# Most of the latent projection as seven half-block products, between those of the gate group, and the sums of w_out run on into the latent heads

## The chip, the core and the metric

The kernel runs on one core of a Trainium2 chip, in one launch. The metric is the device time of the whole kernel in microseconds; runs of one kernel agree within about 0.1 us here. The core has TensorE (matmuls into PSUM banks of 128 x 512 float32), VectorE, ScalarE, GpSimd (POOL in the profile) and SyncE (SP), which issues most transfers. All transfers run on the core's 16 DMA engines.

## The reference

One decoder layer on 512 tokens of width 2048: a combined input projection of the normalized x, eight latent-attention heads and eight forgetting-attention heads, gated with SiLU, an output projection and a normalized residual.

```
h = _rms_norm(x, g_pre)
proj = h @ w_in
(q_lat, kv_lat, k_rope_raw, gate_mla,
 fq, fk, fv, f_logit, gate_fox) = jnp.split(proj, split_points, axis=-1)
o_mla = _mla_branch(q_lat, kv_lat, k_rope_raw, g_q, w_uq, g_kv, w_ukv, cos, sin) * jax.nn.silu(gate_mla)
o_fox = _fox_branch(fq, fk, fv, f_logit, b_forget) * jax.nn.silu(gate_fox)
o = jnp.concatenate([o_mla, o_fox], axis=-1) @ w_out
return x + _rms_norm(o, g_post)
```

The first 768 columns of w_in give q_lat, the next 512 kv_lat. Both are RMS-normalized over their columns and go through w_uq and w_ukv to the queries, keys and values of the latent heads. Everything is float32.

## The kernel before

**Arithmetic.** Each float32 operand is split into a rounded high part (ScalarE) and the low remainder (VectorE), and a product is three matmuls: high x high, high x low, low x high (`mm3`, lines 128 to 131).

**Weights.** All weights pass through one list of chunks of 128 x 1024 values. `chunk(i)` issues the load of chunk i + 4 on SP's queue and queues the split of chunk i + 2 (`divide`, lines 227 to 235: `whi` on ScalarE, `wlo` on VectorE). There are three buffers each for the raw chunk (loads from line 221, or from line 212 for prepared sums), `whi` and `wlo`. So two chunks can stand ready ahead of TensorE and three more be loaded.

**Side work.** `todo` is a list of closures that `pump` takes from while a projection runs: `rate` closures after each block of 128 rows. `wait(n)` puts n empty ones in, `drain` empties the list. `later` is a second list, taken from at every third call of `behind`. Each engine runs its instructions in one order, which the framework's scheduler sets when the program is built, by and large that of the program.

**Seven products.** The latent heads' gate group (1024 columns, tag "m") and the output projection (two groups of 1024 columns, 0 and 1) are each computed as a 2 x 2 block product with seven half-size products, p1, p2, p4, q6, g5, g7 and g3, in the manner of Strassen and Winograd. That needs sums of weight blocks (t4 to t7) and of blocks of x (or of the heads' outputs).
- The weight sums are made by DMA alone, from DRAM to DRAM: `sum_blocks` lists them in `bg` (16 for each group), and `add_step` (lines 273 to 283) issues one step: an accumulating transfer on POOL's queue (line 278), a copy on SP's queue (line 281), and a mark of 64 bytes that ties the next step to TensorE's progress (line 283). `behind` takes a step after every `pace` row blocks of the projections that call it; 7 for the forgetting heads, 6 for the latents, 7 in the latent heads.
- The sums of x are made in `x_steps` while the forgetting heads are projected, split, and put away to DRAM on POOL's queue (`put_away`, line 841). They are fetched back on SP's queue (`fetch`, line 847) beside the product before the one that uses them (`side`).
- `product` (lines 859 to 890) runs one of the seven. The left operand (x or its sums) is the stationary side, a weight half block of 512 columns the moving one; two PSUM banks hold the 256 tokens of a half.

**Order.** (1) x is transposed and split, the forgetting heads are projected in four pairs, their attention pumped beside (up to 407 us). (2) The latents: five groups of 256 columns, plain products over 16 row blocks (`proj_T`, tile `l`, 407 to 523 us): a block of weights of 128 columns against all 512 tokens, so the result stands with columns on partitions. After each group `latent` squares and scales its two parts; after the third and the fifth `latent_scale` turns the summed squares into a row of factors, by eight small matmuls (line 1073), a square root, diagonals (lines 422 and 423), and a matmul that spreads them (lines 431 and 432); then each part is scaled (line 1087). (3) The gate group's seven products (tiles `ga` to `gd`, 523.6 to 603.7 us), the splits of the ten normalized latents pumped beside (`part_latents`, lines 1110 to 1114), then transposes of the gates (line 1147). (4) The latent heads in four pairs (from 603.7 us). (5) The output projection's fourteen products.

All these tiles of 128 x 2 x 512 live in one pool of 28 slots.

## Time and profile before

| | us |
|---|---|
| median of 3 runs | 913.7 (913.68 to 913.78) |
| profiled execution, span from first to last instruction | 912.0 |
| TensorE busy | 903.8 |
| VectorE busy | 601.1 |
| ScalarE busy | 409.3 |
| latent groups, first to last matmul | 407.2 to 523.4 |
| gate group's products, first to last matmul | 523.6 to 603.4 |

Groups of instructions stand as line, engine, operation, tiles, shapes and count, then busy us and mean ns of one, then the engine's idle time before them and what ended it. A row of the order of time is start, length, engine, line. A row of stretches has the stretch, its length, then busy us (and instructions) of TensorE, of its weight loads, VectorE, ScalarE and POOL, then the granted clock, the busy share of the DMA engines and GB/s. A row of waits is who waited for whom: total, times, longest. A row of transfers ends in KB each and the median us to landing; a row of one tile has min/median/max ns and the first and last start. Matmuls are pipelined: a row's length covers part of the next one's, so their price is the distance between starts.

### The profile page before, as it was taken

How to read it: one execution, taken by the hardware profiler on the slowest of the kernel's cores; microseconds unless marked ns; L12 is line 12 of the kernel's file. 1: busy time of each engine (PE TensorE's matmuls, PEld its weight loads, DVE VectorE, ACT ScalarE, POOL GpSimd, SP SyncE). 2: the span in 40 equal slices, each digit the busy share in tenths (PEclk: the TensorE clock that was granted, in tenths of full speed). 3: DMA queues.
4: the chain of work that ended last, by engine and by line, in shares of the span. 5: the costliest groups of instructions: out<-in, count | busy, mean ns of one | idle time of the engine just before them, and what ended most of it. 6: DMA issues, size and time to landing. Idle time of an engine off the chain costs nothing.

```text
span 912.0 us, 12253 instructions
## 1 busy us (share of the span) xinstructions
PE 903.8 (99%) x4460; PEld 767.2 (84%) x4460; DVE 601.1 (66%) x1042; ACT 409.3 (45%) x731; POOL 77.3 (8%) x101
## 2 busy tenths in 40 slices
PE   9999999999999999999999999999999999999997
PEld 8988888898889888888888888888888888888885
DVE  4477779447366674673644556778978895876686
ACT  6772434243223442342533354644454465644474
POOL 1001101011112010111220100000000000000021
PEclk9999999999999999999999999999999999999998
DMA  9368876877788878987999998877422146787868
GB/s 304 92 186 205 210 193 183 213 185 185 202 228 251 231 171 251 248 240 174 293 320 285 269 318 307 296 223 175 102 77 71 47 149 215 238 323 225 275 192 253
DMA packets 119808, 196.20 MB, mean 215 GB/s; under 512 B 15650, under 2 KB 67388, under 8 KB 119748
## 3 DMA queue, kind: packets, MB, share of 16 engines
q1 hardware_dynamic: 103556, 152.03, 50.7%
q0 software_dynamic: 15456, 43.00, 22.8%
q8 instruction: 35, 0.57, 0.2%
q10 hardware_dynamic: 736, 0.40, 0.2%
q14 instruction: 25, 0.20, 0.1%
HBM read 175.45 MB, written 70.27 MB: 269 GB/s over the span
## 4 chain that ended last, share of the span: by engine, by line
PE 94%; DMA 2%; DVE 1%; ACT 1%; issue 0%; SPq 0%; ACTq 0%
PE fv L526 4%; PE l L129 4%; PE l L131 4%; PE l L130 4%; PE fg L129 3%; PE fq L131 3%; PE fq L129 3%; PE fq L130 3%; PE fg L130 3%; PE fg L131 3%; PE fk L130 3%; PE fk L129 3%; PE fk L131 3%; PE sm L565 3%; PE fv L130 2%; PE fv L131 2%
## 5 line engine op out<-in xcount | busy, mean ns | idle before, releaser
L234 DVE TENSOR_TENSOR wlo<-raw,whi 128x1024 fp32r<-128x1024 f32 (+3 forms) x193 | 228.3, 1185 | 182.0 <-ACT whi L233 173.8
L233 ACT CAST whi<-raw 128x1024 fp32r<-128x1024 f32 (+3 forms) x193 | 197.2, 1023 | 277.2 <-PE fk L130 45.6
L129 PE MATMUL l<-h,whi 128*128 128x512 f32 x160 | 63.3, 396 | 0.0
L131 PE MATMUL l<-h,wlo 128*128 128x512 f32 x160 | 62.4, 390 | 0.0
L130 PE MATMUL l<-h,whi 128*128 128x512 f32 x160 | 62.4, 390 | 0.0
L129 PE MATMUL fq<-h,whi 128*128 128x512 f32 x128 | 52.6, 411 | 0.0
L129 PE MATMUL fg<-h,whi 128*128 128x512 f32 x128 | 50.4, 394 | 0.0
L131 PE MATMUL fq<-h,wlo 128*128 128x512 f32 x128 | 50.3, 393 | 0.0
L130 PE MATMUL fq<-h,whi 128*128 128x512 f32 x128 | 50.1, 391 | 0.0
L129 PE MATMUL fk<-h,whi 128*128 128x512 f32 x128 | 50.0, 391 | 0.0
L130 PE MATMUL fg<-h,whi 128*128 128x512 f32 x128 | 50.0, 391 | 0.0
L131 PE MATMUL fg<-h,wlo 128*128 128x512 f32 x128 | 49.9, 390 | 0.0
L130 PE MATMUL fk<-h,whi 128*128 128x512 f32 x128 | 49.8, 389 | 0.0
L131 PE MATMUL fk<-h,wlo 128*128 128x512 f32 x128 | 49.8, 389 | 0.0
L131 PE MATMUL fv<-whi,h 128*128 128x256 f32 (+1 forms) x128 | 39.5, 309 | 0.0
L130 PE MATMUL fv<-wlo,h 128*128 128x256 f32 (+1 forms) x128 | 39.5, 309 | 0.0
L129 PE MATMUL fv<-whi,h 128*128 128x256 f32 (+1 forms) x128 | 39.5, 309 | 0.0
L526 PE MATMUL fv<-whi,h 128*128 128x456 f32 x128 | 37.7, 378 | 0.0
L278 POOL DMA_DIRECT2D t<-in_w_out_dram x16 | 18.7, 1167 | 207.4 <-DMA t<-in_w_out_dram 207.1
L131 PEld LDWEIGHTS l<-h,wlo 128*128 128x128 f32 x160 | 30.0, 188 | 6.4
L129 PEld LDWEIGHTS l<-h,whi 128*128 128x128 f32 x160 | 30.0, 188 | 5.9
L130 PEld LDWEIGHTS l<-h,whi 128*128 128x128 f32 x160 | 30.1, 188 | 5.8
(473 smaller groups left out, 2208.0 us busy)
## 6 DMA issues: line engine op xcount, KB each, us to landing
raw<-in_w_in_dram SPq DMA_DIRECT2D x84, 512.0 KB
t<-in_w_out_dram SPq DMA_DIRECT2D x32, 512.0 KB
raw<-t SPq DMA_DIRECT2D x32, 512.0 KB
raw<-in_w_out_dram SPq DMA_DIRECT2D x24, 512.0 KB
t<-in_w_out_dram POOLq DMA_DIRECT2D x16, 512.0 KB, 8.0
t<-t POOLq DMA_DIRECT2D x16, 512.0 KB, 8.0
awaymg<-smg POOLq DMA_DIRECT2D x12, 512.0 KB, 7.4
bmg<-awaymg SPq DMA_DIRECT2D x12, 512.0 KB
```

Source lines behind the costliest of these rows:

```text
L129: pe.matmul(o, ah, bh, start=first, stop=False, **kw)
L130: pe.matmul(o, ah, bl, start=False, stop=False, **kw)
L131: pe.matmul(o, al, bh, start=False, stop=last, **kw)
L233: act.copy(hi[:, :m], raw[:, :m])
L234: dve.tensor_tensor(out=lo[:, :m], in0=raw[:, :m], in1=hi[:, :m].bitcast(F32), op=ALU.subtract)
L278: pool.dma_start(to.rearrange("p (k c) -> p k c", k=2), second, accum_op=ALU.add)
L526: pe.matmul(banks[t][:, :n], a[k][:, tss[t]], b[:, j, :], start=k == 0 and m == 0, stop=k == NK - 1 and m == 2,)
L565: pe.matmul(s[:, :nn], a[:, qs], c[:, :nn], start=(i == 0), stop=(i == len(pairs) - 1))
```

## The change

The first 1024 of the 1280 latent columns become a group "l" of seven products like the gate's. Its left operands are the same blocks and sums of x as the gate's, held until both groups have used them. `turned` makes the weight block of 128 columns the stationary side and 256 tokens the moving one, so that the result has columns on partitions as before. The last 256 latent columns stay a plain group and come first. p1, p2 and p4 of the two groups alternate; then q6, g5, g7, g3 of the latents run, then those of the gate. The latents' squares, statistics, rows, scalings and splits are pumped beside the latents' g3 and the gate's q6 and g5 (two closures after each block), with shorter waits between them. The list of weight sums grows by 16 steps, which come first; the pace is 6 row blocks for a step up to the plain latent group, 16 in the products (which now take steps too, through `paced`), and 2 in the latent heads. The fetches of x sums run beside p2 and q6 to g5 of the latents and p4 of the gate.

```diff
-    state = {"loaded": 0, "divided": 0, "tiles": 0, "turn": 0, "step": -1, "pace": 7}
+    state = {"loaded": 0, "divided": 0, "tiles": 0, "turn": 0, "step": -1, "pace": 6}
...
-    lat = [add_chunks(w_in, [(0, 256 * p, 256)], NK, 4, 256) for p in range(5)]
+    lat = add_chunks(w_in, [(0, 1024, 256)], NK, 4, 256)
...
+    AT = {"l": 0, "m": O_GM}
+
+    def in_block(g, j, h, c):
         k = 2 * j + 8 * h
-        return w_in[0, k * P : (k + 2) * P, O_GM + 512 * c : O_GM + 512 * (c + 1)].rearrange("(k p) c -> p k c", p=P)
-
-    sum_blocks("m", gate_block)
+        off = AT[g] + 512 * c
+        return w_in[0, k * P : (k + 2) * P, off : off + 512].rearrange("(k p) c -> p k c", p=P)
+
+    for g in "lm":
+        sum_blocks(g, lambda j, h, c, g=g: in_block(g, j, h, c))
     add_products(
-        [(n, "m") for n in ("p1", "p4", "p2", "q6", "g5", "g7", "g3")],
-        lambda g, h, c: add_chunks(w_in, [(0, O_GM + 512 * c, 512)], 8, 2, 512, 8 * h),
+        [
+            *((n, g) for n in ("p1", "p2", "p4") for g in "lm"),
+            *((n, g) for g in "lm" for n in ("q6", "g5", "g7", "g3")),
+        ],
+        lambda g, h, c: add_chunks(w_in, [(0, AT[g] + 512 * c, 512)], 8, 2, 512, 8 * h),
     )
...
+            for f in range(2):
+                c = slice((2 * t + f) * P, (2 * t + f + 1) * P)
+                mm3(
+                    o[t][:, f * HALF : (f + 1) * HALF], hi[:, j, c], lo[:, j, c], *parts(kk),
+                    first and kk == 0 and f == 0, last and kk == 7, skip_group_check=True,
+                )
...
                 pump(rate)
+                paced(hi)
...
+    def latent_row(j):
+        make_row(accs[:, j, :], f"lr{LAT[j][0]}", *lat_diag[j])
...
+    def latent_part(i):
+        j = int(i >= 6)
+        dve.tensor_tensor(out=raw(i), in0=raw(i), in1=accs[:, j, :], op=ALU.mult)
+        latents[i] = split(raw(i), f"ln{i}")
...
+    def lat_sum(to, o, add, op=ALU.add):
+        for t in range(2):
+            dve.tensor_tensor(out=to[t], in0=fold(o[t]), in1=add[t], op=op)
...
+    state["pace"] = 16
+    A, A2 = ([proj_bank(f"g{n}{t}") for t in range(2)] for n in "lm")
+    product("p1", "l", x_wide(0, 0), A, True, True, 2, turned=True)
...
+    product("p1", "m", x_block(0, 0), A2, True, True, 2)
...
+    product("p2", "l", x_wide(1, 0), A, False, True, 2, side=fetches("q6", "m"), turned=True)
...
+    product("p2", "m", x_block(1, 0), A2, False, True)
...
+    product("p4", "l", x_wide(1, 2), B, True, True, turned=True)
+    lat_sum(lat_block(0, 1), B, pl)
+    product("p4", "m", x_block(1, 2), B2, True, True, side=fetches("g5", "m"))
...
+    drain()
...
+    product("q6", "l", sums_wide("q6"), C, True, True, side=fetches("g7", "m"), turned=True)
...
+    product("g5", "l", sums_wide("g5"), G, True, True, side=fetches("g3", "m"), turned=True)
+    lat_sum(lat_block(1, 1), G, pl, ALU.subtract)
+    product("g7", "l", sums_wide("g7"), C, False, True, turned=True)
+    lat_sum(lat_block(1, 1), C, lat_block(1, 1))
+    lat_less(lat_block(0, 1), C)
+    for i in range(4):
+        todo.append(lambda i=i: latent(i, raw(i)))
+    product("g3", "l", sums_wide("g3"), G, False, True, turned=True)
+    lat_sum(lat_block(1, 0), G, lat_block(1, 0))
+    for i in range(4, 8):
+        todo.append(lambda i=i: latent(i, raw(i)))
+    wait(2)
+    todo.append(lambda: latent_stats(0))
+    todo.append(lambda: latent_stats(1))
+    wait(6)
+    todo.append(lambda: latent_row(0))
+    todo.append(lambda: latent_row(1))
+    wait(3)
+    for i in range(10):
+        todo.append(lambda i=i: latent_part(i))
+    C, G = ([proj_bank(f"g{n}m{t}") for t in range(2)] for n in "cd")
+    product("q6", "m", operand("q6", "m"), C, True, True, 2)
...
+    product("g5", "m", operand("g5", "m"), G, True, True, 2)
...
-    part_latents()
-    product("g7", "m", operand("g7", "m"), C, False, True)
+    product("g7", "m", operand("g7", "m"), C, False, True, 2)
...
-    state["pace"] = 7
+    state["pace"] = 2
```

More of the change, by code (lines that the diff above doesn't have):

```diff
@@ L857, in operand, with product @@
         return parts
-    def product(name, g, parts, o, first, last, rate=1, at=None, held=0, side=()):
+    def product(name, g, parts, o, first, last, rate=1, at=None, held=0, side=(), turned=False):
         side = deque(side)
@@ L1163, in tile_hybrid_layer @@
-    c11 = slot("gc11")
-    scaled_copy(c11, A, 0)
-    C = [proj_bank(f"gc{t}") for t in range(2)]
-    product("q6", "m", operand("q6", "m"), C, True, True, side=fetches("g7", "m"))
+    state["pace"] = 16
+    A, A2 = ([proj_bank(f"g{n}{t}") for t in range(2)] for n in "lm")
+    product("p1", "l", x_wide(0, 0), A, True, True, 2, turned=True)
+    pl = slot("lp")
+    for t in range(2):
+        act.copy(pl[:, t, :], A[t])
+    pl = [fold(pl[:, t, :]) for t in range(2)]
+    product("p1", "m", x_block(0, 0), A2, True, True, 2)
@@ L1187, in tile_hybrid_layer @@
             f()
-    qnh, qnl = zip(*qn)
-    knh, knl = zip(*kn)
+    qnh, qnl = zip(*(latents[i] for i in range(6)))
+    knh, knl = zip(*(latents[i] for i in range(6, 10)))
     for p in range(4):
```

104 lines of the change are left out of this document (54 added, 50 removed).

## The prediction

> **What bounds the kernel now.** I read the page first, then who TensorE waited for, then its order of time and the stretches around the change.
>
> ```profile
> span 912.0 us, 12253 instructions
> ...
> PE 903.8 (99%) x4460; PEld 767.2 (84%) x4460; DVE 601.1 (66%) x1042; ACT 409.3 (45%) x731; POOL 77.3 (8%) x101
> ...
> PEclk9999999999999999999999999999999999999998
> DMA  9368876877788878987999998877422146787868
> ...
> PE 94%; DMA 2%; DVE 1%; ACT 1%; issue 0%; SPq 0%; ACTq 0%
> ```
>
> TensorE is busy for 903.8 of 912.0 us at full clock, and the chain that ended last is TensorE for 94%. So the time is the sum of matmul spacings, and an edit counts by what it does to that sum or by a hole it makes in it. The list of TensorE's own waits shows how few holes there are:
>
> ```profile
> PE mix L1306 <- ACT scaler L1305: 1.9, 1, 1.9
> PE warm L148 <- DVE warm L143: 1.1, 1, 1.1
> PE xt L394 <- DMA xa<-in_x_dram: 0.6, 1, 0.6
> PE gmt L1147 <- DVE gc L1131: 0.4, 1, 0.4
> ```
>
> Between the first and the last few microseconds there is one hole, of 0.4 us, at the gate transposes. The digits of DMA say that around the latent and gate stages (slices 18 to 24, 410 to 570 us) its engines are nearly full: that is where to look for a new bound.
>
> **The matmuls removed and added.** Four of the five latent groups go: 4 groups x 16 row blocks x 2 outputs x 3 terms = 384 matmuls that stream 512 columns. Seven products come: 7 x 8 x 2 x 2 x 3 = 672 matmuls that stream 256, since turned, each weight block of 128 columns is the stationary side and half the tokens (256) the moving one. A matmul's shown length overlaps its neighbours, so the price is the distance of starts:
>
> ```profile
> 448.06 0.39 PE L129 MATMUL l<-h,whi 128*128 128x512 f32 x1
> ...
> 453.50 0.39 PE L129 MATMUL l<-h,whi 128*128 128x512 f32 x1
> ...
> 173.55 0.28 PE L129 MATMUL fv<-whi,h 128*128 128x256 f32 x1
> ...
> 196.58 0.40 PE L129 MATMUL fg<-h,whi 128*128 128x512 f32 x1
> ...
> L131 PE MATMUL fv<-whi,h 128*128 128x256 f32 x64 | 18.1, 283 | 0.0
> ...
> 419.17 0.28 PE L129 MATMUL pvf<-phf,fv0h 128*128 128x256 f32 x1
> ...
> 419.51 0.40 PE L129 MATMUL l<-h,whi 128*128 128x512 f32 x1
> ```
>
> The latent matmuls: 24 starts in 453.50 - 448.06 = 5.44 us, 0.2267 us each. The value projection of the second head pair has the very form that comes, 128 x 128 stationary and 256 moving, back to back: 3 x 64 = 192 starts in 196.58 - 173.55 = 23.03 us, 0.120 us each. That is not half of 0.2267: if 256 more columns cost 0.1067 us, each matmul pays 0.0133 us besides. So removed 384 x 0.2267 = 87.0 us, added 672 x 0.120 = 80.6 us, **gain 6.4 us**. In other words, an eighth of the streaming saved (384 x 0.2133 / 8 = 10.2 us) and 288 more fixed costs (3.8 us) paid. The bounds: three lone matmuls of 256 (419.17 to 419.51) stand 0.113 apart, which would give 672 x 0.113 = 75.9 and a gain of 11.1; no row of this form is slower than 0.120. I take 0.120, the row with 192 of them in a run.
>
> The Trainium skill, "TensorE: Matmul & The Clock Gate", section Back-to-back issue gap, has N/2.4 ns + 2.5 ns per matmul, which would price the pair at 215.8 and 109.2 ns and the gain at an estimated 9.5 us. The Trainium skill's "Perfetto Trace Analysis", section Matmuls, speaks against the edit: larger matmuls are more efficient than smaller ones. This trace agrees with that direction and has the larger price, 13.3 ns for each matmul instead of 2.5; the row decides.
>
> **Weights, splits, evacuation.** The seven products read 28 chunks of 1024 columns where 16 were read: 12 more loads of 512 KB, 12 more roundings on ScalarE and 12 more subtractions on VectorE (some 1.0 and 1.2 us each by the rows of L233 and L234 below). TensorE takes a chunk in 24 x 0.120 = 2.88 us instead of 24 x 0.2267 = 5.44. A chunk is prepared two ahead, so the two engines' 2.2 us fit into 5.8 us of lead: cost nothing, covered by TensorE's own work, and up to 12 x 2.2 = 26 us if there were no lead. The evacuations (4 copies, 12 additions of 128x512) run while the next product uses other banks: p1, p2 and p4 alternate with the gate group's, and q6, g5, g7, g3 alternate two bank pairs as the gate products do now. Nothing, but they load VectorE.
>
> **Statistics and splits of the latents, moved behind g3 into the gate group's last four products.** Here VectorE must do in 4 x 48 x 0.2267 = 43.5 us what it did over a longer stretch:
>
> ```profile
> 562.00:594.00 32.00, 32.00 (x143) 26.48 (x142) 22.45 (x26) 17.59 (x23) 0.00 (x0) 1.00 0.86 307
> 594.00:606.00 12.00, 11.64 (x61) 9.48 (x60) 10.93 (x15) 6.54 (x9) 0.00 (x0) 1.00 0.59 154
> 606.00:640.00 34.00, 34.00 (x188) 29.33 (x187) 24.64 (x45) 14.95 (x28) 1.99 (x2) 1.00 0.78 215
> ...
> L234 DVE TENSOR_TENSOR wlo<-raw,whi 128x1024 fp32r<-128x1024 f32 (+1 forms) x16 | 18.7, 1173 | 11.0 <-ACT whi L233 10.8
> L233 ACT CAST whi<-raw 128x1024 fp32r<-128x1024 f32 (+3 forms) x193 | 197.2, 1023 | 277.2 <-PE fk L130 45.6
> L1087 DVE TENSOR_TENSOR lat<-lat,ls 128x512 f32<-128x512 f32 x10 | 6.4, 688 | 0.0
> L1064 DVE TENSOR_TENSOR ls<-ls,lq 128x512 f32<-128x512 f32 x4 | 2.8, 692 | 4.0 <-ACT lq L1061 4.0
> ...
> 535.87 0.95 PE L1073 MATMUL lbk<-ones,ls 128*128 128x1 f32 x8
> ...
> L423 DVE TENSOR_SCALAR lrkdl<-ident,lrkl x4: 281/282/286, 543.7 to 544.3; 128x128 fp32r<-128x128 f32 x4
> ```
>
> VectorE's fourth number of the first two rows: 22.45 + 10.93 = 33.4 us busy in those 44 us, the splits of the ten latents among it. To it come ten scalings (6.4), four additions of squares (2.8), two sets of diagonals (2 x 4 x 0.28 = 2.2) and four 128x512 operations (two row copies, two sums of g3; 4 x 0.69 = 2.8): 47.6 us for 43.5, over by 4.1. What runs over can slip into the next stretch, where VectorE has 34.0 - 24.6 = 9.4 us free. Second, the row sums: from lbk's matmuls (535.87) to the end of lrkdl (544.6) took 8.7 us, and where there were six pumps of one row block each, there are now six at two per row block, 3 x 1.36 = 4.1 us. If TensorE stands at the row matmul in that order, it waits 4.6 us, and the gate products behind it in its queue with it. Bounds: 0 to 4.1 + 4.6 = 8.7 us. Which value? The gate transposes of before are such a place (VectorE behind with 10.93 of 12 us busy), and they waited 0.36 us; three such places (statistics, rows, transposes) are **1.1 us**, which I take.
>
> **Transfers.** The rows of the stretches, the last two numbers being the busy share of the DMA engines and GB/s:
>
> ```profile
> 60.00:410.00 350.00, 350.00 (x1753) 300.16 (x1752) 226.91 (x425) 124.16 (x214) 40.41 (x47) 1.00 0.80 213
> 432.00:480.00 48.00, 48.00 (x215) 39.80 (x214) 26.39 (x36) 22.08 (x35) 11.63 (x18) 1.00 0.98 305
> 480.00:522.00 42.00, 42.00 (x190) 34.86 (x189) 21.01 (x35) 14.37 (x21) 5.93 (x6) 1.00 1.00 272
> 522.00:546.00 24.00, 24.00 (x111) 19.96 (x111) 11.89 (x23) 14.23 (x22) 0.00 (x0) 1.00 0.95 317
> 640.00:760.00 120.00, 120.00 (x683) 104.19 (x682) 101.05 (x214) 61.32 (x137) 0.81 (x1) 1.00 0.29 90
> ...
> awayog<-sog POOLq DMA_DIRECT2D x6, 512.0 KB, 11.7
> L841 POOL DMA_DIRECT2D awayog<-sog x6: 533/744/1007, 441.7 to 470.3; - x6
> t<-t POOLq DMA_DIRECT2D x5, 512.0 KB, 8.7
> ...
> ACT whi L233 <- DMA raw<-in_w_in_dram: 23.3, 7, 7.2
> SPq L281 <- DMA t<-whi: 66.5, 22, 10.9
> L212 SPq DMA_DIRECT2D raw<-t x32: 319/320/423, 771.5 to 849.0; - x32
> L129 PE MATMUL mv<-whi,kn x64: 277/283/386, 619.1 to 735.6; 128*128 128x256 f32 x64
> ```
>
> The weight sums grow from 48 to 64 steps of two 512 KB transfers (a copy on SP's queue, an accumulation on POOL's). Counted by row blocks, the pace makes 240 / 6 = 40 steps to the end of the one plain latent group, 112 / 16 = 7 in the fourteen products, 20 in the latent heads at one per two blocks. The latent and gate sums (33 steps) are issued 198 blocks in, before the products. Five more steps against 0.80 DMA share before 410 us cost nothing: a chunk has 5.44 us there. The twenty in the heads meet a share of 0.29, where one accumulation lands 8.7 us after its issue; the last is issued near the end of mv (735.6) and its sum loaded only after the first of the raw<-t at 771.5: nothing, while 20 us of cover are left. SP waits for its little marks (66.5 us in all), loads queued behind; with 16 blocks between steps a mark has some 22 us, and the 10.9 us wait has no cause in the products.
>
> The products themselves: p1 of both groups takes 11.5 + 10.9 = 22.4 us and asks for 8 loads, up to 14 operands put away through POOL's queue (pumped at two per block, earlier spread up to 470.3 us) and 3 transfers of sums, 25 x 0.524 MB = 13.1 MB. At the 305 GB/s of 432 to 480 us that takes 43 us. The put-aways may be late at no cost; the loads may not. Their lead is two prepared chunks and three raw ones, 5 x 2.8 = 14 us. With a share of 0.95 and eight transfers a product at 2.72 us a chunk, the gate stage of before (522 to 546) left no hole, so I take 0; bounds 0 to 13.3 us (first rival). The sixteen fetches of x sums move from p1, p4, p2, q6 and g5 of the gate to p2 and p4, then q6 and g5 of the latents; they stand on SP's queue among the loads, each wanted a product later at the earliest, as now.
>
> **Sum.** 912.0 - 6.4 + 1.1 = 906.7 us of span. The median of the runs (913.7) stands 1.7 us above the profiled span: **908.4 us**. Unhindered 907.3; with the lone spacing 0.113 it is 913.7 - 11.1 = 902.6.
>
> **Rivals.**
> 1. *Transfers become the bound, and it is slower.* Loads, operand put-aways and fetches share the DMA engines evenly, so a load waits for all that was issued before it. At the 317 GB/s of 522 to 546 us a transfer takes 0.524 / 0.317 = 1.65 us. Lateness, transfers less TensorE's time: p1 of both groups 25 x 1.65 - 22.4 = 18.9; p2 of the latents (loads, fetches, one of the sums: nine) 14.9 - 11.5 = 3.4; p2 of the gate and p4 of the latents (five each) give back 2.6 and 3.2; p4 of the gate, q6 and g5 of the latents (nine each) add 4.0, 3.4 and 3.4. Together 27.3, less 14 of lead: 13.3 us, or 913.7 - 6.4 + 13.3 = 920.6 at the worst; with a quarter of the put-aways (14 x 1.65 / 4 = 5.8 us) left behind the loads it is 914.8. I set it at the middle, **918**. It decides once the loads are 14 + 6.4 us late. For it: 0.98 to 1.00 of DMA from 432 to 522, put-aways of 11.7 us, ScalarE waiting up to 7.2 us for a raw chunk. Against: no hole there now, and steps of sums almost three times rarer. The Trainium skill, "DMA: Bandwidth & Descriptors", section Queues, rings and completion order: each engine goes round robin over the queues that have work. By that rule POOL's put-aways would take a share from SP's loads as long as they last, which is what this rival needs; no row here shows the shares within one engine.
> 2. *VectorE becomes the bound of the last four products.* Its surplus and the row wait fall on TensorE with 6.4 of their 8.7 us: **913.7**, no change. For it: 47.6 us of work in 43.5. Against: weights split ahead of the latents' work, 9.4 us free behind.
> 3. *The small matmuls are dearer or cheaper than their row*: 0.113 apart gives **902.6**; the other end, that halving the moving side doesn't pay (0.1295 apart is break-even), is not in any row.
>
> **Chances.** Forecast 0.62, first rival 0.18, second 0.14, third 0.06. A change under 0.2% (1.8 us) can't be told from none with this kernel's runs. Faster: forecast and third, 0.68; same: the second, 0.14; slower: the first, 0.18. The likeliest case's own range is 906 to 911; with the upper part of the second and most of the first it is 905.5 to 918, which leaves out the cheap spacing and the worse half of the transfers (0.06 + 0.09) and a little at the ends.
>
> **What would show it.** 672 matmuls of 256 columns 0.120 us apart; a TensorE busy time near 897.5; from the first product to the last gate product (80.6 + 76.2 us of matmuls) a stretch of 157 us without the transposes. Wrong if TensorE waits for whi or wlo inside p1, p2, q6 or g5 (first rival: then ScalarE waits for raw), or for the row's diagonals and for VectorE's wlo in the gate group's q6 to g3 (second), or if POOL's last accumulation lands after 771 us and SP stands before a raw<-t.

## The result, and the profile after

| | before | after |
|---|---|---|
| median of 4 runs on one chip, us | 913.7 (913.68 to 915.84) | 936.6 (931.42 to 940.07) |
| profiled execution, span, us | 912.0 | 929.6 |
| time after / time before | | 1.0235, interval 1.0211 to 1.0259 |

The changed kernel is slower by 2.4%. Its profiled execution is the fastest of its four (931.42); the median lies 5 us above, and the runs spread over 8.6 us where those of before spread over 2.2. How much is lost varies from run to run, and only this one execution has a profile: the 5 us that the median lies higher stand in no trace. The kernel before varies too, more than the 0.1 us of its first three runs: in the jobs of the experiments its single runs lie between 913.5 and 919.2.

The page of after, the same parts as before:

```profile
span 929.6 us, 13021 instructions
...
PE 905.0 (97%) x4748; PEld 778.8 (84%) x4748; DVE 621.0 (67%) x1066; ACT 423.8 (46%) x747; POOL 93.4 (10%) x117
...
DMA  9377987887988998895999987689999745786868
...
PE 88%; DMA 6%; DVE 3%; ACT 1%; issue 1%; SPq 0%; ACTq 0%; DVEq 0%
```

TensorE's share of the chain fell from 94 to 88%, and transfers have 6% of it. The digits of DMA read 9 from some 630 to 720 us, where before they fell from 4 to 1. TensorE's own waits, where before the longest inside the kernel was 0.4 us:

```profile
PE gcm L130 <- DVE wlo L234: 4.9, 3, 2.3
PE gm L130 <- DVE wlo L234: 2.6, 2, 1.9
PE mq L129 <- DVE mv0l L121: 2.6, 1, 2.6
PE gl L131 <- DVE wlo L234: 2.6, 2, 1.9
```

Three places: the gate's g7 (`gcm`, which q6 writes too, but the three waits end between 587 and 597 us), the first products (`gm`, `gl`), and the latent heads (`mq`). To find what each costs I take the first matmul of a tile as a mark and read the distances, in the profiled executions:

| us | before | after | expected of the matmuls |
|---|---|---|---|
| start to first latent matmul | 407.2 | 407.6 | |
| plain latent group (`l` to `gl`) | | 27.9 | |
| p1 and p2 of both groups (`gl` to `gbl`) | | 56.2 | 192 x 0.120 + 96 x 0.2267 = 44.8 |
| p4, and q6 to g3 of the latents (`gbl` to `gcm`) | | 68.5 | 480 x 0.120 + 48 x 0.2267 = 68.5 |
| the gate's last four (`gcm` to `mq`) | | 54.9 | 48.9 |
| all from `l` to the heads | 196.5 | 207.5 | 196.5 - 6.4 = 190.1 |
| heads and the output's p1, p2 (`mq` to `ob`) | 180.1 | 186.0 | 180.1 |
| to the end | 128.2 | 128.5 | |

(48.9 is what is left of 190.1 after the three stages above it: 192 x 0.2267 = 43.5 and 5.4 for the transposes and the small matmuls there.) So the 17.6 us between the spans are -6.4 as expected, +11.4 in p1 and p2, +6.0 in the gate's last four, +5.9 in the heads, and 0.7 at the ends. (The 48.9 rests on the -6.4; gate_pump_one, below, bears it out with 48.2 and no hole.)

**The matmuls came as predicted.** Two rows of the order of time of after, 35 starts apart with no hole between:

```profile
472.11 0.28 PE L129 MATMUL gl<-h,whi 128*128 128x256 f32 x1
...
476.31 0.28 PE L131 MATMUL gl<-h,wlo 128*128 128x256 f32 x1
```

4.20 / 35 = 0.120 us, and the stage without holes takes its 68.5 us to the tenth. TensorE's busy time is 905.0 and not 897.5: in three stretches of 3.4 us behind holes the granted clock is 0.50 (last section), which makes 5.1 of these 7.5 us. Stretches of after (columns as in the prediction: TensorE, loads, VectorE, ScalarE, POOL, clock, DMA share, GB/s):

```profile
442.00:453.00 11.00, 11.00 (x70) 9.73 (x69) 10.13 (x15) 6.47 (x10) 3.74 (x8) 1.00 1.03 377
453.00:465.00 12.00, 10.12 (x48) 8.40 (x49) 5.75 (x8) 4.98 (x7) 1.60 (x3) 0.86 1.03 405
465.00:476.00 11.00, 8.22 (x64) 7.61 (x64) 7.42 (x9) 5.36 (x8) 1.76 (x2) 1.00 1.05 360
476.00:488.00 12.00, 10.55 (x43) 8.35 (x43) 5.38 (x5) 6.22 (x7) 0.00 (x0) 0.86 0.97 341
...
584.00:596.00 12.00, 7.93 (x36) 5.72 (x34) 10.24 (x16) 5.71 (x9) 1.13 (x1) 1.00 0.65 153
...
640.00:660.00 20.00, 16.82 (x80) 14.14 (x79) 12.21 (x33) 7.65 (x19) 2.88 (x4) 0.91 1.05 262
```

**p1 and p2.** With POOL's put-aways beside the loads the DMA engines are full (1.03 to 1.05) at 360 to 405 GB/s. ScalarE then stands for the raw chunk (14.7 us in eight waits between 435 and 492 us), TensorE for the chunk's low part:

```profile
463.76 1.05 ACT L233 CAST whi<-raw 128x1024 fp32r<-128x1024 f32 x1 [4.16 <-DMA raw<-in_w_in_dram]
...
476.90 1.05 ACT L233 CAST whi<-raw 128x1024 fp32r<-128x1024 f32 x1 [4.18 <-DMA raw<-in_w_in_dram]
```

The raw chunk of the first of these waits was also issued late: SP stood 8.0 us, up to 455.4, at the mark of a step (line 283), until ScalarE had written the `whi` that it reads, with the load queued behind it (issued at 455.7, landed 7.9 us later). spread_put_away, below, shows what that stand is worth.

**The gate's last four.** DMA has room (0.65), VectorE has not (10.24 of 12 us busy): it takes the latents' scalings and splits in a lump ahead of `wlo`. VectorE in the order of time:

```profile
584.19 1.89 DVE L121 TENSOR_TENSOR ln<-lat,ln 128x512 fp32r<-128x512 f32 x3
586.00 1.22 DVE L234 TENSOR_TENSOR wlo<-raw,whi 128x1024 fp32r<-128x1024 f32 x1
587.13 1.89 DVE L1115 TENSOR_TENSOR lat<-lat,ls 128x512 f32<-128x512 f32 x3
588.94 1.88 DVE L121 TENSOR_TENSOR ln<-lat,ln 128x512 fp32r<-128x512 f32 x3
590.74 0.68 DVE L1115 TENSOR_TENSOR lat<-lat,ls 128x512 f32<-128x512 f32 x1
591.35 1.22 DVE L234 TENSOR_TENSOR wlo<-raw,whi 128x1024 fp32r<-128x1024 f32 x1
```

Between the two `wlo` stand 4.2 us of latent work (587.13 to 591.35); TensorE's waits of 1.18 and 2.32 us end at 587.27 and 592.62.

**The heads.** The chain of waits of after:

```profile
635.67 8.61 DMA t<-whi
...
644.37 0.84 ACT whi L233
...
645.23 0.31 DVE wlo L234
...
646.11 0.43 DVE mv0l L121
```

And ScalarE in the order of time there:

```profile
644.37 0.83 ACT L233 CAST whi<-raw 128x768 fp32r<-128x768 f32 x1 [4.00 <-DMA t<-whi]
```

A mark of 64 bytes took 8.6 us. It reads a `whi` buffer, so ScalarE's next high part waited 4.0 us for the buffer, and VectorE's work behind it (`mv0l`), on which TensorE stood for 2.6 us, came late. Whether the marks did it, or DMA engines that are full anyway, was the question for the experiments.

### The profile page after: what moved, and what is told of

Its sections match the earlier page's. It is cut to its first block, busy times and chain, and to the rows that moved or that the text cites. A ratio compares the mean times of both kernels' runs of the same rounds, so it can differ in the third digit from the quotient of the medians.

```text
span 929.6 us, 13021 instructions
## 1 busy us (share of the span) xinstructions
PE 905.0 (97%) x4748; PEld 778.8 (84%) x4748; DVE 621.0 (67%) x1066; ACT 423.8 (46%) x747; POOL 93.4 (10%) x117
## 3 DMA queue, kind: packets, MB, share of 16 engines
q1 hardware_dynamic: 105060, 166.71, 54.8%
## 4 chain that ended last, share of the span: by engine, by line
PE 88%; DMA 6%; DVE 3%; ACT 1%; issue 1%; SPq 0%; ACTq 0%; DVEq 0%
PE fv L536 4%; PE fg L129 3%; PE fq L131 3%; PE fq L129 3%; PE fq L130 3%; PE fg L131 3%; PE fg L130 3%; PE fk L131 3%; PE fk L129 3%; PE fk L130 3%; DMA raw<-in_w_in_dram 2%; PE sm L575 2%; PE fv L131 2%; PE fv L130 2%; PE fv L129 2%; PE sf L575 2%
## 5 line engine op out<-in xcount | busy, mean ns | idle before, releaser
L234 DVE TENSOR_TENSOR wlo<-raw,whi 128x1024 fp32r<-128x1024 f32 (+3 forms) x205 | 242.6, 1186 | 173.0 <-ACT whi L233 169.4
L233 ACT CAST whi<-raw 128x1024 fp32r<-128x1024 f32 (+3 forms) x205 | 209.1, 1021 | 296.4 <-PE fk L130 45.9
L130 PE MATMUL fk<-h,whi 128*128 128x512 f32 x128 | 49.8, 389 | 0.0
L131 PE MATMUL fk<-h,wlo 128*128 128x512 f32 x128 | 49.8, 389 | 0.0
L129 PE MATMUL mq<-ln,whi 128*128 128x512 f32 x72 | 29.8, 414 | 3.2 <-DVE mv0l L121 2.6
L278 POOL DMA_DIRECT2D t<-t x16 | 13.4, 836 | 190.3 <-DMA t<-in_w_out_dram 144.7
L592 ACT ACTIVATE pm<-sm,stm 128x128 f32<-128x128 f32 (+3 forms) x32 | 16.9, 528 | 29.0 <-DVE stm L590 28.9
L592 ACT ACTIVATE pf<-sf,stf 128x128 f32<-128x128 f32 (+3 forms) x32 | 16.9, 528 | 28.8 <-DVE stf L590 28.4
L130 PE MATMUL mq<-ln,whi 128*128 128x512 f32 x72 | 28.8, 400 | 0.0
L131 PE MATMUL mq<-ln,wlo 128*128 128x512 f32 x72 | 28.7, 398 | 0.0
```

The source lines that it names most:

```text
L129: pe.matmul(o, ah, bh, start=first, stop=False, **kw)
L130: pe.matmul(o, ah, bl, start=False, stop=False, **kw)
L131: pe.matmul(o, al, bh, start=False, stop=last, **kw)
L233: act.copy(hi[:, :m], raw[:, :m])
L234: dve.tensor_tensor(out=lo[:, :m], in0=raw[:, :m], in1=hi[:, :m].bitcast(F32), op=ALU.subtract)
L278: pool.dma_start(to.rearrange("p (k c) -> p k c", k=2), second, accum_op=ALU.add)
```

## The experiments

All distances are those of the table above, in the one profiled execution of each run, between starts rounded to 0.1 us; ratios are to the kernel before, on the same chip in the same job (its medians there 914.0 to 916.0).

| run | start of `l` | p1, p2 | p4 to g3 | gate's four | heads | span | ratio, interval |
|---|---|---|---|---|---|---|---|
| after | 407.6 | 56.2 | 68.5 | 54.9 | 186.0 | 929.6 | 1.0235, 1.0211 to 1.0259 |
| heads_no_steps | 439.9 | 55.9 | 68.6 | 54.0 | 180.1 | 956.8 | 1.0492, 1.0468 to 1.0516 |
| old_steps_in_heads | 407.5 | | | | 190.5 | 922.1 | 1.0081, 1.0061 to 1.0102 |
| early_put_away | 407.7 | 49.1 | 68.7 | 56.6 | 185.7 | 924.2 | 1.0127, 1.0109 to 1.0144 |
| gate_pump_one | 408.1 | 56.8 | 69.2 | 48.2 | 185.9 | 924.7 | 1.0155, 1.0105 to 1.0206 |
| steps_on_pool | 478.4 | 62.2 | 73.3 | 59.1 | 232.7 | 1070.1 | 1.1649, 1.1562 to 1.1736 |
| spread_put_away | 408.7 | 55.3 | 69.5 | 54.9 | 189.4 | 934.2 | 1.0237, 1.0217 to 1.0257 |
| mended_paces | 410.7 | 52.2 | 70.3 | 48.1 | 182.6 | 920.3 | 1.0089, 1.0066 to 1.0111 |
| marks_ahead | 407.8 | 55.2 | 69.7 | 54.8 | 188.2 | 932.1 | 1.0215, 1.0196 to 1.0234 |
| old_steps_marks_ahead | 406.9 | | | | 180.3 | 911.4 | 1.0034, 1.0002 to 1.0066 |
| early_pump_one_marks | 408.8 | 47.8 | 70.2 | 48.3 | 192.1 | 923.6 | 1.0136, 1.0096 to 1.0177 |
| early_pump_one_marks_5_16_3 | 417.0 | 48.7 | 70.5 | 49.8 | 185.4 | 927.8 | 1.0169, 1.0114 to 1.0224 |
| heads_vector_relieved | 409.1 | 50.2 | 68.5 | 48.4 | 190.3 | 923.0 | 1.0080, 1.0048 to 1.0111 |
| heads_steps_later | 407.1 | 51.8 | 68.5 | 47.8 | 192.9 | 924.6 | 1.0196, 1.0140 to 1.0252 |
| heads_both | 407.4 | 48.1 | 69.3 | 48.4 | 201.0 | 930.6 | 1.0147, 1.0093 to 1.0201 |
| steps_into_output | 407.3 | 47.4 | 69.3 | 48.6 | 190.3 | 919.4 | 1.0052, 1.0033 to 1.0070 |
| relieved_steps_into_output | 407.5 | 47.3 | 69.6 | 48.5 | 187.7 | 917.0 | 1.0038, 1.0021 to 1.0055 |
| relieved_steps_thinner | 407.6 | 46.6 | 70.1 | 50.0 | 184.2 | 915.4 | 1.0032, 1.0012 to 1.0053 |

### One cause at a time

**heads_no_steps**: the changed kernel with more steps ahead of the latents, so that none is left for the heads.

```diff
-    state = {..., "step": -1, "pace": 6}
+    state = {..., "step": -1, "pace": 4}
```

> The changed kernel with one step of the weight sums for every 4 row blocks up to the plain latent group instead of 6, so that 60 of 64 steps are out before the products and none is left for the latent heads. Theory: in the latent heads SP stands before a copy until its 64-byte mark has landed (8.6 us once), and the loads of w_uq queue behind it; this costs 5.9 us from the first mq matmul to the first ob matmul (186.0 us against 180.1 before the change). Without steps there that distance is 180 to 181 and the kernel 4 to 7 us faster than the changed one. Rival: the heads are late for another reason (VectorE still behind from the gate group); the distance stays near 186. Second rival: the DMA engines are too full before 407 us for 20 more steps, and the first plain latent matmul comes 3 us or more later than 407.6.

The heads fall to 180.1, the time of before, though the gate's four leave VectorE as late as in the changed kernel (54.0). So the heads' 5.9 us are the steps. The price comes up elsewhere, dearer, as the second rival had it: 32.3 us ahead of the latents. Stretches of heads_no_steps and of after there, and TensorE's waits of heads_no_steps:

```profile
60.00:407.00 347.00, 328.39 (x1605) 280.38 (x1604) 202.68 (x371) 110.23 (x186) 58.23 (x64) 0.97 0.99 256
```
```profile
60.00:407.00 347.00, 347.00 (x1738) 297.66 (x1737) 223.82 (x420) 121.73 (x210) 45.73 (x52) 1.00 0.87 228
```
```profile
PE pvf L130 <- DVE plf L121: 9.1, 3, 7.3
PE fv L130 <- DVE wlo L234: 4.8, 1, 4.8
```

The DMA share goes from 0.87 to 0.99 and TensorE loses 18.6 of 347 us of busy time.

**old_steps_in_heads**: the kernel before, with its own 48 steps moved so that about as many stand in the heads as after the change.

```diff
-    state = {..., "step": -1, "pace": 7}
+    state = {..., "step": -1, "pace": 10}
...
-    state["pace"] = 6
+    state["pace"] = 10
...
-    state["pace"] = 7
+    state["pace"] = 2
```

> The kernel before with its own 48 steps paced so that 20 of them fall into the latent heads (one for every 10 row blocks, then one for every 2). Nothing else of the change is in it. Theory of the mark: the distance from the first mq to the first ob matmul grows from 180.1 to between 183 and 187 us and the kernel by the same 3 to 6 us (917 to 920). Rival: the heads have cover for the steps, as the prediction had it, and the kernel stays at 913.7 within 1 us.

The heads go from 180.1 to 190.5, with none of the latents' seven products there: the steps alone cost 10 us in this execution, more than the 3 to 6 expected, and 7 us at the median (922.9 against 916.0).

**early_put_away**: the put-aways drained beside the plain latent group.

```diff
-    proj_T(lat, [(lb[i], P, two[i]) for i in range(2)], hh, hl)
+    proj_T(lat, [(lb[i], P, two[i]) for i in range(2)], hh, hl, rate=2)
```

> The changed kernel with two closures instead of one pumped after each block of the plain latent group, so that the heads' operands are made and put away some 8 to 11 us earlier, when the DMA engines are at 0.32 (430 to 442 us). Theory (put-aways and loads share the DMA engines): p1 and p2 of both groups, 56.0 us from the first matmul to p4's first where 44.8 us of matmuls are, shrink to 47 to 51, and the kernel is 5 to 9 us faster than the changed one. Rival (the loads are late because each raw buffer comes free too late, ScalarE and VectorE being held by the operand work): 56 or longer, since the same work is only crowded at another place.

p1 and p2 fall from 56.2 to 49.1: 7.1 of their 11.4 us go with the put-aways that stood among the loads (ten of the fourteen are now issued before 434 us). The edit takes the making of these operands along: VectorE's work in the stage falls from 36.9 to 27.0 us, and SP's stand of 8.0 us at the mark is gone too. **spread_put_away** left them there and thinned them (one closure a block in p1 of both groups and p2 of the latents):

> The changed kernel with one closure instead of two pumped in p1 of both groups and in the latents' p2, so that the operands put away come at half the rate over four products instead of two. Theory (the DMA engines are full there, and bytes can only be moved to where the engines have room): starting early helped because there was room before 442 us; spreading later helps less, since p2 brings fetches: 51 to 55 us from the first latent p1 matmul to the first latent p4 matmul (56.2 in the changed kernel, 49.1 with the early start). Rival (it is the burst alone that hurts): 46 to 50.

Only 0.9 us are won (55.3), and the whole stays where it was, though here too SP stands at the mark for only 2.5 us. So the stand at the mark was hardly the main cost: what helps here is to have the transfers, and the work that makes them, ahead of the loads, not thinner among them.

**gate_pump_one**: one closure a block in the gate's q6, g5 and g7.

```diff
-    product("q6", "m", operand("q6", "m"), C, True, True, 2)
+    product("q6", "m", operand("q6", "m"), C, True, True)
```

> The changed kernel with one closure instead of two pumped after each block of the gate's q6, g5 and g7. Theory (VectorE has more to do than the four products last, and its scalings and splits of the latents come in one lump ahead of the weights' subtractions): the stretch from the gate's q6 to the first mq matmul, 54.9 us where 43.5 us of product matmuls are (46.0 before the change), shrinks to 47 to 50, the kernel by 4 to 8 us. Rival (VectorE simply has too much to do there, whatever the order): 53 or more, as gates slip behind. Second rival (raw chunks come late there because of the DMA engines): unchanged 55.

The gate's four fall from 54.9 to 48.2, with no wait of TensorE left in them. All ten scalings and ten splits of the latents stay in the stage, no longer in a lump ahead of `wlo`: their place in the queue cost the 6 us. VectorE's whole work in the stage is smaller too, 42.4 instead of 47.5 us, since what comes last there, mostly four multiplications of the gates (2.7 us), now slips behind the first `mq`; the heads take no longer for it (185.9).

### Marks or bytes

In the heads the marks stand in the way: SP waits for one ahead of each copy, with loads queued behind, and ScalarE waits for the buffer that one reads. If only that costs, the marks can be taken from SP or issued earlier.

**steps_on_pool** (copy and mark on POOL's queue) and **mended_pool** (that with both repairs above):

```diff
-            nc.sync.dma_start(to.rearrange("p (k c) -> p k c", k=2), first)
+            pool.dma_start(to.rearrange("p (k c) -> p k c", k=2), first)
...
-            nc.sync.dma_start(bg[n + 1][0][0:1, 0:16], mark)
+            pool.dma_start(bg[n + 1][0][0:1, 0:16], mark)
```

> The changed kernel with the copies and the marks of the weight sums issued on POOL's queue instead of SP's; same steps, same paces, same bytes. Theory of the mark: SP no longer stands before a copy until a mark lands, so the loads of w_uq and w_ukv are issued in time and the distance from the first mq to the first ob matmul falls from 186.0 to 180 to 182 us. Rival: what makes the heads late is the number of bytes (20 steps make the DMA engines full), and then the distance stays at 184 or more, because the loads land late wherever the steps are issued.

> The same mends of the pumps, with the paces of the changed kernel (6, 16, 2) and the copies and marks on POOL's queue. If SP's standing is the cause in the heads: 180 to 182 there, and with 48 to 50 and 48 at the other two places a span of 908 to 912, faster than the kernel before by 0 to 4 us. If bytes are the cause: 184 or more in the heads and a span of 913 or more.

Both are far slower (mended_pool 1059 us, ratio 1.158), by waits of their own. What POOL waited for in steps_on_pool:

```profile
POOL t L278 <- DMA t<-in_w_out_dram: 148.7, 29, 7.3
POOL t L281 <- DMA t<-whi: 100.6, 19, 8.4
POOL t L283 <- ACT whi L233: 75.5, 7, 21.3
```

POOL now stands for each mark, and the put-aways and accumulations are in the same queue behind it. The runs say nothing on marks against bytes, and which of these waits costs the most was not separated.

**marks_ahead** and **old_steps_marks_ahead**: the mark of step n + 2 is issued behind the copy of step n, in the changed kernel and in old_steps_in_heads.

```diff
-        if n + 1 < len(bg):
-            nc.sync.dma_start(bg[n + 1][0][0:1, 0:16], mark)
+        for k in (n + 1, n + 2) if n < 0 else (n + 2,):
+            if k < len(bg):
+                nc.sync.dma_start(bg[k][0][0:1, 0:16], mark)
```

> The changed kernel with each mark issued one step earlier (the mark of step n + 2 behind the copy of step n), so that it has two steps' time to land before SP reaches the copy that waits for it; the same bytes at the same places. Theory of the marks (in the latent heads SP stands for the mark's landing, and the loads of w_uq and w_ukv queued behind it come late): the latent heads fall from 186.0 to 180 to 183 us, and the whole to 931 to 934. Theory of the bytes (the transfers of the twenty steps crowd out the loads, wherever SP stands): heads 185 to 187, whole 935 to 938.

> The kernel before with its paces moved to 10, 10 and 2 (as in old_steps_in_heads, where the latent heads took 190.5 us instead of 180.1), and each mark issued one step earlier. Marks: heads 180 to 184, whole 913 to 917. Bytes: heads 189 to 191, whole 921 to 924.

A split answer. In the order of before the earlier mark takes the whole 10 us away (190.5 to 180.3), at the same bytes, but the profiled execution is the fastest of ten: seven lie at 913.2 to 918.6 us and three at 923.3 to 925.4, as slow as without the earlier mark. It stands at an edge. Stretches of old_steps_marks_ahead and of old_steps_in_heads:

```profile
640.00:720.00 80.00, 79.80 (x453) 69.35 (x452) 65.97 (x142) 38.59 (x90) 13.31 (x14) 1.00 1.01 242
```
```profile
640.00:720.00 80.00, 76.76 (x428) 66.35 (x427) 61.46 (x129) 35.02 (x79) 11.95 (x12) 0.98 0.99 235
```

The first has the fuller DMA engines, 1.01 for 80 us, and TensorE loses 0.2 us there; the second loses 3.2 at 0.99. So a full share alone does not make a hole.

In the changed kernel the earlier mark does nothing (186.0, then 188.2). ScalarE's waits from 604 to 800 us show what came in the marks' place; of after, then of marks_ahead:

```profile
ACT whi L233 <- DMA t<-whi: 8.1, 2, 4.1
...
ACT whi L233 <- DMA raw<-in_w_ukv_dram: 2.1, 1, 2.1
```
```profile
ACT whi L233 <- DMA raw<-in_w_ukv_dram: 9.0, 2, 7.0
...
ACT whi L233 <- DMA t<-whi: 0.3, 1, 0.3
```

The wait for marks fell from 8.1 to 0.3 us, and the wait for a raw chunk rose from 2.1 to 9.0. The chain of waits of marks_ahead, and that of early_pump_one_marks (below), show such chunks, 14.5 and 12.5 us from issue to landing:

```profile
638.22 14.46 DMA raw<-in_w_ukv_dram
652.78 1.05 ACT whi L233
653.85 1.23 DVE wlo L234
```
```profile
608.32 12.54 DMA raw<-in_w_uq_dram
620.95 1.05 ACT whi L233
...
623.25 0.61 DVE mq L124
```

### Do the repairs add up?

**mended_paces** (early_put_away, spread_put_away and gate_pump_one, paces 5, 16 and 3), **early_pump_one_marks** (early_put_away, gate_pump_one, marks_ahead), and the latter with paces 5, 16 and 3:

> The changed kernel with all three places mended by order alone: two closures pumped in the plain latent group, one in p1, p2 and in the gate's q6, g5 and g7, and the steps of the sums at 5 row blocks up to the plain latent group, 16 in the products and 3 in the heads (13 of them there instead of 20). Theory: 48 to 50 us for p1 and p2 of both groups, 48 for the gate's last four, 182 to 184 for the heads; start of the plain latent group 407 to 412 us, since one step for 4 blocks cost 32 us there and one for 6 only 0.4. Sum: a span of 910 to 918, close to the kernel before. Rival (the DMA engines are full from the sums to the heads, and what is taken away at one place comes back at another): 920 or more.

> The changed kernel with the put-aways drained beside the plain latent group at two a block, one closure a block in the gate's q6, g5 and g7, and the marks one step earlier. If the three repairs add up as measured apart: 407.6 to the latents, 28 for the plain group, 49.1 for p1 and p2, 68.6 to the gate's q6, 48.2 for the gate's last four, 181 for the heads, 128.5 behind: 911 of span, about 913 in the runs, which is the kernel before. Without an effect of the marks: heads 186, 918. Rival (each repair hands its transfers to the next stage): p1 and p2 back at 52 or more and the gate's last four at 50 or more, 918 to 925.

> As early_pump_one_marks, with the paces 5, 16 and 3 instead of 6, 16 and 2: more steps before the latents, fewer in the heads. Marks: the heads have nothing left to gain from fewer steps (180 to 181), while the start of the latents slips to 410.7 as in mended_paces: 914 to 916, slower than pace 2. Bytes: heads 182.6 as in mended_paces, about 918, and no slower than early_pump_one_marks.

They do not: the span of early_pump_one_marks is 923.6 where 911 was the sum. p1 and p2 and the gate's four stay mended (47.8 and 48.3, 15.0 us less than in after), but the heads give 6.1 us of it back: 192.1 instead of 186.0. mended_paces, with fewer steps in the heads, has 182.6 there, and 52.2 in p1 and p2: a span of 920.3, as its rival had it. More steps ahead of the latents move the loss to their start (417.0), which was in neither expectation.

**heads_vector_relieved** takes work off VectorE ahead of the heads, **heads_steps_later** takes the steps out of the stretch from the gate's q6 to the end of the first pair of heads, **heads_both** does both.

```diff
-    for i in range(10):
+    for i in range(6):
         todo.append(lambda i=i: latent_part(i))
...
-    knh, knl = zip(*(latents[i] for i in range(6, 10)))
+    for i in range(6, 10):
+        todo.append(lambda i=i: latent_part(i))
```
```diff
+    state["pace"] = 99
     C, G = ([proj_bank(f"g{n}m{t}") for t in range(2)] for n in "cd")
...
+        if p == 1:
+            state["pace"] = 1
         c = mla[p]
```

> early_pump_one_marks (heads 192.1 us, span 923.6) with VectorE relieved before the latent heads: the two row copies go to ScalarE, and scaling and split of the four key and value latents are pumped beside the first pair's queries instead of the gate's last product: 1.4 + 5.5 us of VectorE's work less before 603. The steps stay. If VectorE's lateness is the cause (a): heads 180 to 183, span 911 to 915. If the steps near the first pair are enough (b): heads 188 or more, span 919 to 924.

> early_pump_one_marks with no steps from the gate's q6 to the end of the first pair of heads, and one for each row block from the second pair on (19 steps in some 135 us; VectorE's work as it was). (a): heads 187 or more, as the first weights are issued as late as before, span 918 to 924. (b): heads 180 to 183 if a step for each block in the later pairs does no harm there, span 911 to 915.

> heads_vector_relieved and heads_steps_later together. Both theories: heads 180 to 182, span 910 to 913, the kernel before at best. If the heads still take 185 or more, the steps themselves are the cost wherever they stand in the heads.

VectorE's lateness falls as the cause: with it relieved the heads take 190.3. But (b) as I had put it falls too: with the first pair free of steps the loss isn't gone, it has moved (192.9). heads_both takes 201.0, the most of all: by its own expectation the steps are the cost wherever they stand in the heads. Stretches of heads_steps_later:

```profile
620.00:640.00 20.00, 20.00 (x117) 17.52 (x116) 17.00 (x34) 8.74 (x19) 2.84 (x3) 1.00 0.89 230
640.00:660.00 20.00, 20.00 (x117) 17.42 (x116) 18.09 (x37) 9.45 (x20) 4.46 (x5) 1.00 1.03 230
660.00:680.00 20.00, 16.43 (x96) 14.18 (x94) 8.77 (x20) 5.26 (x14) 1.56 (x2) 1.00 1.05 246
680.00:700.00 20.00, 13.60 (x60) 11.52 (x61) 13.37 (x33) 9.14 (x20) 4.02 (x4) 0.75 1.05 256
```

TensorE is full up to 660 and loses 10 us between 660 and 700, behind the stretch in which the DMA share first passes 1. That pointed to density, whatever the place, though old_steps_marks_ahead speaks against density alone. The last three runs tried it: **steps_into_output** (early_pump_one_marks, a step for three blocks in the heads, then one for two blocks in the output projection's first two products, and what is left ahead of the third), **relieved_steps_into_output** (that on heads_vector_relieved) and **relieved_steps_thinner** (a step for four blocks in the heads). The paces of the last, which also issues what is left ahead of p2:

```diff
-    state["pace"] = 2
+    state["pace"] = 4
...
-    assert state["step"] > len(bg) and not later
+    assert not later
+    state["pace"] = 2
```

> early_pump_one_marks (heads 192.1, span 923.6), with a step for every three row blocks in the latent heads instead of two and the rest in the output projection's first two products, one for two row blocks there. If the density of the steps is the cost: heads (with those two products) 180 to 184, span 911 to 916. If each step costs about half a microsecond wherever it stands: heads 189 or more, or TensorE waiting in the output projection's first products, span 920 to 925.

> heads_vector_relieved (heads 190.3, span 923.0) with the steps as in steps_into_output. Density: heads 180 to 183, span 910 to 914. Each step costs: heads 188 or more, span 919 to 923. Against steps_into_output it shows what VectorE's relief is worth once the steps are thin: 0 to 2 us.

> As relieved_steps_into_output with a step for every four row blocks in the heads, so that eight or more stand in the output projection's first products. Density: heads 180 to 182, or the loss moves behind them (a share of DMA near 1 from 735 to 770 and TensorE waiting there): span 910 to 916. Each step costs: 919 to 923.

The heads go 190.3, 187.7, 184.2 as the steps thin and VectorE is relieved. The first is where the rival had it (189 or more), the second lies between the two theories, the third has the loss behind the first pairs, which its expectation allowed for. At one step for four blocks, TensorE has no hole in the heads before 772 us. Stretches of relieved_steps_thinner, and of before:

```profile
640.00:740.00 100.00, 100.00 (x579) 87.20 (x578) 85.66 (x172) 49.52 (x110) 7.94 (x8) 1.00 0.63 154
740.00:780.00 40.00, 37.80 (x184) 31.25 (x183) 23.20 (x47) 19.02 (x38) 4.79 (x5) 0.96 0.99 279
```
```profile
640.00:740.00 100.00, 100.00 (x579) 87.17 (x578) 85.73 (x174) 49.05 (x110) 0.81 (x1) 1.00 0.25 75
```

What is left of the loss sits at 740 to 780, where the remaining steps meet the loads of the output projection at a share of 0.99: ScalarE stands 7.1 us for a raw chunk of w_out, and TensorE 2.2 us for what ScalarE has behind it. These rows also give an estimate of a step's price: seven more accumulations, with their copies, raise the share by 0.38 of 100 us, so each step takes some 38 / 7 = 5.4 us of all the DMA engines.

The best kernel with the change takes 917.6 us at the median, 0.3% more than the kernel before. No version here beats it. Nor was the whole gain ever collected ahead of the heads: from `l` to the heads steps_into_output takes 193.2 us, 3.3 less than before instead of 6.4.

## Why the prediction was wrong

**Right: the matmuls.** The term of -6.4 us came whole as a price: 0.120 us for each matmul of 256 columns and 68.5 us for the stage without holes.

**Failed: "Transfers ... so I take 0".** p1 and p2 cost 11.4 us, within the bounds I had given (0 to 13.3), by the first rival's mechanism: loads beside put-aways, ScalarE standing for raw chunks. The evidence I set against it was a stretch without holes at a share of 0.95; that stretch had no put-aways. early_put_away bears the mechanism out for 7.1 us of the 11.4; how much of that is the transfers and how much the work that makes them is not separated. The rival's lateness in p4, q6 and g5 did not come: that stage lost nothing. The Trainium skill's round robin over queues ("DMA: Bandwidth & Descriptors", Queues, rings and completion order) pointed that way; no run here shows the shares inside an engine.

**Failed: the choice of 1.1 us for VectorE.** The bounds were 0 to 8.7, the stage lost 6.0. I compared amounts of work (47.6 us in 43.5) and took the low end because what runs over could slip behind. But the order was fixed: at two closures a block the latents' parts stand ahead of `wlo`, which TensorE needs, not behind it. gate_pump_one has the same closures at half the rate and loses nothing: there some 5 us of VectorE's work do slip behind the stage, as I had supposed. The error was to weigh a sum where the place in the queue decides.

**Failed: "twenty steps in the heads ... nothing, while 20 us of cover are left", and the marks with "no cause in the products".** This was in no rival, and it cost 5.9 us. I priced when the last sum lands, not what twenty steps do to the stretch they stand in. And a mark did hold up SP in the products, 8.0 us in p1, though by spread_put_away little of the loss there hangs on it. The stretch of after with 17 accumulations:

```profile
624.50:722.00 97.50, 93.61 (x525) 80.85 (x524) 76.32 (x150) 42.57 (x93) 16.18 (x17) 0.98 0.97 231
```

By the estimate of 5.4 us for a step 17 of them are 92 us, and the 0.25 of before make 24 more: 116 us of transfers for 97.5. The row itself has 0.97, 94.6 us, so the steps took (94.6 - 24) / 17, some 4 us each. By either price the engines are full, and a mark took 8.6 us there. My own row showed 0.29 for 640 to 760; by the 5.4 it had room for about 85 / 5.4 = 16 steps in 120 us at the most, without any spare for the loads' landing. That the steps cost the 5.9 us is shown (heads_no_steps, old_steps_in_heads); that they cost it through the full engines alone is not, since old_steps_marks_ahead ran as full without loss.

**Failed: the form of the range.** Its upper end, 918, held one rival at a time. All three went wrong together, since each is another stage with its own full resource (the DMA engines, VectorE, the DMA engines again): 11.4 + 6.0 + 5.9. The sum of the bounds that I had, 907.3 + 13.3 + 8.7 = 929.3, was the upper end, and the heads, which had no bound at all, carry it past that. One sum is also wrong by itself: a quarter of the put-aways left behind the loads gives 913.7 - 6.4 + 5.8 = 913.1, not 914.8, which hardly moves the middle of 918.

**Left open.** With early marks the loads carry the loss in the changed kernel, while in the order of before nothing does in most runs, though as many steps stand there (17 accumulations in the heads of each) and the DMA engines are as full; what makes the one recover and the other not was not settled. Nor was a place found for the sixteen added steps: ahead of the latents, in the heads and in the output projection they cost more than the matmuls gave back, in every version. Whether a form of the change without them (sums made on an engine) would pay was not tried.

## What to carry to other kernels

Price moved transfers by the stretch they land in: so many of them, times what each takes of all the DMA engines, plus the share already there; near 1, loads and even the smallest marks can come late, and work that was free can become a hole. Whether it does hangs on how early they are issued, too: old_steps_marks_ahead lost nothing at a share of 1.01 once the marks went out a step sooner, and seven of its ten runs were as fast as that or nearly so. In an in-order queue the place of the work decides, not its sum: spread what is pumped beside matmuls so that what TensorE needs next is never behind a lump. Where a change leans on several resources that are each nearly full, add their upper bounds; here relief in one stage did not even come through whole, since the next ones gave part of it back.

## What the runs showed of the hardware

**A hole can cost more than its length.** After TensorE's wait of 1.88 us that ended at 457.80, in the order of time of after:

```profile
458.82 0.42 PE L131 MATMUL gm<-whi,h 128*128 128x512 f32 x1
...
459.47 0.63 PE L130 MATMUL gm<-wlo,h 128*128 128x512 f32 x1
459.89 0.63 PE L131 MATMUL gm<-whi,h 128*128 128x512 f32 x1
460.32 0.63 PE L129 MATMUL gm<-whi,h 128*128 128x512 f32 x1
```

The distance of starts, 0.23 us up to there, goes to 0.43 (459.47 to 460.32, two distances of 0.42 and 0.43), from 459.05 for 3.41 us, with a granted clock of 0.50. The same follows the hole of 2.63 us in the heads (from 646.79), and two holes of only 0.69 and 0.76 us that end at 478.00 and 479.26 (from 479.53). It does not follow the other hole of 1.88 us, which ends at 467.24, nor those of 1.18, 2.32 and 1.38 us in the gate's last four (clock 1.00). So the length of a hole alone does not decide. The three slow stretches begin 20.48 and 167.25 us apart, 6 and 49 times 3.413 us. The Trainium skill, "TensorE: Matmul & The Clock Gate", Part 1: The HAM clock gate, has a half clock after an idle window of about 3.4 us that runs free of the kernel. The half rate, the length and the even spacing agree with this trace; but here holes of 0.7 to 2.6 us were enough.

**A full share is not one rate.** The share was 1.03 at 405 GB/s with loads and put-aways (453 to 465), and 1.03 to 1.05 at 230 to 262 GB/s with the steps in the heads: copies and accumulations from DRAM to DRAM take more of the engines for each byte (by the estimate above some 5 us for the 1.05 MB of a step, where loads and put-aways of that size at 405 GB/s take 2.7).
